# A fourth tile in the turn of right sides of the Strassen steps of a feed-forward block

## The chip, the cores and the metric

The kernel runs on one core of one Trainium2 chip. The metric is the device time of one execution in microseconds (us), as the median of several runs. The core's engines are named as the profile names them: PE multiplies matrices (PEld loads its weights), DVE and POOL work on vectors, ACT evaluates functions and copies, and SP issues the DMA transfers; each runs its own list of instructions in order.

## The reference

Two layers of a diffusion backbone run for two request groups of 1024 and 128 tokens that share all weights. Each layer is a mixer (a recurrence and a pooling in the first, latent attention in the second) and then a feed-forward block with a squared ReLU:

```python
D_MODEL = 1024
D_FF = 4 * D_MODEL

def sq_relu_mlp(h, w1, w2):
    return jnp.square(jax.nn.relu(h @ w1)) @ w2

...
        xs = xs + ms[5] * sq_relu_mlp(modulate(xs, p['g_ffn'], ms[3], ms[4]), p['ffn_w1'], p['ffn_w2'])
```

The change lies in the product with `w2`, which is computed once in each of the two layers.

## The kernel before

All tokens lie transposed: 1152 columns (1024 and 128) in NQ = 4 chunks of Q = 288. Every f32 factor is split into a high part, rounded to the multiplier's own f32r format, and a low part that is the rest; `mm3` (L165 to L168) then makes three matmuls, high by high, high by low and low by high. `split` (L157 to L163) makes the two parts: ACT copies the high part (L162), and DVE or POOL subtracts it to get the low one (L163).

`ffn` runs `up` for the first product, which squares its result and stores it to DRAM as high and low parts (`ad`) and unsplit (`ar`). The second product handles 14 of the 16 blocks of rows in seven **Strassen steps** of two blocks each, and the two others (`PLAIN`) directly. A step forms seven products, in the order of LATE: A11, A12, S3, A22, S2, S1, S4. Each is made for two halves g = 0 and 1, so a step has 14 **tiles** in a row, which are counted here from 0 to 13: A11 is tiles 0 and 1, A12 2 and 3, S3 4 and 5, A22 6 and 7, S2 8 and 9, S1 10 and 11, S4 12 and 13. One tile is 24 matmuls on PE, in four groups of six; each group fills a PSUM bank, which DVE adds to an accumulator (L881; in the first step ACT copies it, L877).

The right side of a tile is four [128, 288] pieces, high and low, in a buffer named `at` (4608 bytes per partition). Tiles 0 to 3, 12 and 13 (A11, A12, S4) are loaded from DRAM by `direct` (L852). Tiles 4 to 11 are sums that POOL makes in place in a tile `fb_b` (`right_sides`, L696), and `split` writes their parts into `at`. The buffers come from one turn, in which 14 tiles take three buffers one after the other:

```python
        four = lambda p, n=3: lambda: p.t([P, 2, 2, Q], F32R, tag="at", bufs=n)
...
        ats = cycle(four(fq))
```

A tile's load or split can begin when PE has finished with the tile that had the buffer before. The two `fb_b` tiles of the next step (L858, 1152 KB each) are loaded when the last splits of this step have read the old ones, and they stand on SP's queue ahead of the loads of tiles 12 and 13.

PE's order is the order of the code. The orders of DVE, ACT, POOL and SP are made when the kernel is built, by a scheduler with a model of the times; on the chip they are fixed. Memory on the left side is a stack: `fb`, then the accumulators, lie where the inputs of the first product lay. Layers 0 and 1 have the same code, with names that end in 0 and 1 (fq0, fq1).

Of the kernel before, what the change touches and what calls it, by code (L numbers as in the profile page):

```python
# [77 lines left out]
def emit(tc, A, O):  # L78
# [216 lines left out]
    def modulate(norm, x, c, hs, l, ffn, lo_eng=(po, ve), inplace=False, spare=None):  # L295
        scl = (sc_ffn if ffn else sc_mix)[l]
        sh0 = 24 if ffn else 0
        hh, hl = hs[c]
        for k in range(KT):
            xn = x[c][:, k, :]  # L300
            sh = lambda g: mod[l][:, sh0 + k, g:g + 1]
            if inplace:
                for a, b, g in groups(c, norm.ch):
                    ve.tensor_scalar(xn[:, a:b], xn[:, a:b], scl[:, k, g:g + 1], sh(g), op0=OP.mult, op1=OP.add)
                split(hh[:, k, :], hl[:, k, :], xn, eng=lo_eng[k % len(lo_eng)])
                continue
            xs = spare.t([P, norm.ch], tag="xn", bufs=2)
            for a, b, g in groups(c, norm.ch):
                ve.scalar_tensor_tensor(xs[:, a:b], xn[:, a:b], scl[:, k, g:g + 1], norm.rs[c][:, a:b],
                                        op0=OP.mult, op1=OP.mult)  # L310
            for a, b, g in groups(c, norm.ch):
                act(hh[:, k, a:b], xs[:, a:b], AF.Identity, bias=sh(g))
            for a, b, g in groups(c, norm.ch):
                ve.scalar_tensor_tensor(hl[:, k, a:b], xs[:, a:b], sh(g), hh[:, k, a:b].bitcast(F32),
                                        op0=OP.add, op1=OP.subtract)
# [402 lines left out]
    def slots_of(pools):  # L718

        while True:  # L720
            for s in pools:
                h = s.t([P, 1024], F32R, tag="hlh", bufs=3 if s is state["wl"] else 2)
                lo = s.t([P, 1024], F32R, tag="hll", bufs=3 if s is state["wl"] else 2)
                for i in range(2):
                    yield h[:, i * 512:(i + 1) * 512], lo[:, i * 512:(i + 1) * 512]
# [10 lines left out]
    def cycle(*makers):  # L736
        while True:
            for f in makers:
                yield f()
# [3 lines left out]
    def ffn(l, x, hs, hclose, tail, slow, then):  # L743

        fq = Scope(f"fq{l}", side="right")
# [5 lines left out]
        four = lambda p, n=3: lambda: p.t([P, 2, 2, Q], F32R, tag="at", bufs=n)  # L751
# [54 lines left out]

        fz = Scope(f"fz{l}", side="right")
        fb = Scope(f"fb{l}")
        raws = cycle(*[from_wp] * 3, lone(fx), lone(fz))
        slots = slots_of([fw, fw, state["wl"], state["wl"], state["wl"]])  # L810
        ats = cycle(four(fq))
        ae = Each(f"acc{l}")
        acc = {n: [ae.t([P, 4, Q]) for _ in range(2)] for n in ("A11", "S3", "A22", "S2", "S1", "S4", "A12")}

# [8 lines left out]
        def collect(name, g):  # L823

            t = {n: a[g] for n, a in acc.items()}
            add = lambda e, o, p, q: e.tensor_tensor(t[o], t[p], t[q], op=OP.add)  # L826
            if name == "A12":
                add(ve, "A12", "A12", "A11")
            elif name == "S3":
                gated(2 * g, 0, t["A12"])  # L830
            elif name == "S2":
                add(ve, "S2", "S2", "A11")
                add(po, "S3", "S3", "S2")
                add(po, "A22", "A22", "S3")
            elif name == "S1":
                add(po, "A11", "S3", "S1")
                add(ve, "S1", "S1", "S2")
                add(po, "S4", "S4", "S1")
                gated(2 * g, 1, t["A22"])
            elif name == "S4":  # L840
                gated(2 * g + 1, 1, t["A11"])
                gated(2 * g + 1, 0, t["S4"])

        todo = [s for s in range(ns) if s not in PLAIN]
        for s in todo[::2]:
# [15 lines left out]
            for name, o in LATE:  # L861
                ws = next(cw)
                for g in range(2):
# [18 lines left out]
                    if end:  # L882
                        collect(name, g)
        ae.close()
        fb.close()
        fp = Scope(f"fp{l}", side="right")
        then()
# [65 lines left out]
    def leave():  # L953
        ht.close()
        h0.close()

    ffn(0, x, hs, leave, Tail(nm, x, spill, lambda c, m: (po, ve)[c // 3], (5,) * 4), slow,
        lambda: hin.extend(chunk_pairs(hx, 4)))
    hs = hin
# [488 lines left out]

    end = Tail(nm, x, done, lambda c, m: ve if c == NQ - 1 else po, (5, 5, 5, 4))
    ffn(1, x, hs, leave, end, lambda *a: iter(()), lambda: None)  # L1450
    gain(NQ - 2)
    gain(NQ - 1)
# [130 lines left out]
```

## Time and profile before

| | |
|---|---|
| median of 3 runs | 2968.59 us (2967.73 to 2974.57) |
| the profiled execution | 2964.8 us |
| its span from first to last instruction | 2962.8 us |
| mean granted TensorE clock | 0.974 |
| busy share of the span | PE 94%, DVE 64%, ACT 46%, POOL 40% |

The profiled execution is one execution, and the rows below are of it. The Strassen steps lie at about 883 to 1212 us in layer 0 and 2590 to 2880 us in layer 1. A granted clock of 1.00 is 2.4 GHz and of 0.50 is 1.2 GHz. "Idle before" in a timeline row is the time for which the engine did nothing before that instruction, with what ended it behind the arrow.

### The profile page before, as it was taken

To read this page: it belongs to the slowest core of one execution; us is meant where nothing else is said; L and a number is where in the kernel's file an instruction comes from. 1 tells how busy PE (TensorE), PEld (TensorE's weight loads), DVE (VectorE), ACT (ScalarE), POOL (GpSimd) and SP (SyncE) were. 2 spreads that over 40 slices of the span, in tenths; PEclk is the share of its full clock that TensorE was granted. 3 is DMA by queue.
4 is the path that set the end of the run, shared out by engine and by line. 5 is a ranking of instruction groups with operands and counts; after the bars stand their busy time and mean duration, and the time that the engine had idled before them with its cause. 6 is when DMAs were issued, how large, how long until landed. Compare 5 with 4: busy or idle time off the path is not lost.

```text
span 2962.8 us, 51575 instructions
## 1 busy us (share of the span) xinstructions
PE 2791.4 (94%) x19896; PEld 2693.8 (91%) x19896; DVE 1910.7 (64%) x3518; ACT 1352.5 (46%) x3143; POOL 1187.8 (40%) x984
## 2 busy tenths in 40 slices
PE   5898799999999999899999999999999999999987
PEld 3886698999999999898999999988999999999987
DVE  5559677665656787875777777776831112377886
ACT  3356243222335222454777777773432223532335
POOL 3544111112157867624333233331011112777775
PEclk7999899999999999999999999999999999999998
DMA  5233414656655554420000000023244444555442
GB/s 225 94 120 103 167 51 166 217 207 215 219 188 175 181 172 158 136 81 21 20 15 21 14 15 23 23 91 109 85 172 156 151 163 151 187 169 173 153 158 88
DMA packets 144941, 372.78 MB, mean 126 GB/s; under 512 B 15944, under 2 KB 49080, under 8 KB 143288
## 3 DMA queue, kind: packets, MB, share of 16 engines
q1 hardware_dynamic: 144696, 369.50, 36.7%
q8 instruction: 156, 2.56, 0.4%
q14 instruction: 89, 0.73, 0.1%
HBM read 260.68 MB, written 108.75 MB: 125 GB/s over the span
## 4 chain that ended last, share of the span: by engine, by line
PE 76%; DVE 9%; DMA 4%; ACT 4%; POOL 3%; issue 3%; SPq 0%; DVEq 0%; ACTq 0%; POOLq 0%
PE ps_b L166 19%; PE ps_b L167 19%; PE ps_b L168 19%; PE pS_o L1145 3%; PE pS_t L1127 3%; DMA fq_at<-dram_t 3%; PE pS_s L166 3%; PE pS_s L168 2%; PE pS_s L167 2%; ACT aw_p L1120 1%; POOL acc_t L826 1%; PE pS_g L166 1%; PE pS_g L168 1%; PE pS_g L167 1%; ACT aw_ph L1131 1%
## 5 line engine op out<-in xcount | busy, mean ns | idle before, releaser
L765 POOL TENSOR_TENSOR fu_r<-fu_r 128x576 f32<-128x576 f32 x128 | 159.9, 1249 | 670.1 <-ACT fu_ah L764 647.3
L167 PE MATMUL ps_b<-ht_t,wl_hlh 128*128 128x288 f32 (+1 forms) x1312 | 404.9, 309 | 13.7 <-DVE ht_t L163 9.1
L166 PE MATMUL ps_b<-ht_t,wl_hlh 128*128 128x288 f32 (+1 forms) x1312 | 407.9, 311 | 7.3 <-ACT ht_t L162 5.0
L168 PE MATMUL ps_b<-ht_t,wl_hll 128*128 128x288 f32 (+1 forms) x1312 | 402.6, 307 | 0.0
L881 DVE TENSOR_TENSOR acc_t<-ps_b,acc_t 128x288 f32<-128x288 f32 x656 | 278.1, 450 | 94.6 <-PE ps_b L168 91.0
L766 DVE TENSOR_TENSOR fu_ah<-fu_r,fu_ah 128x576 fp32r<-128x576 f32 (+1 forms) x128 | 90.2, 705 | 358.9 <-POOL fu_r L765 358.9
L166 PE MATMUL ps_b<-fq_at,wl_hlh 128*128 128x288 f32 x1024 | 308.1, 301 | 12.1 <-DMA fq_at<-dram_t 12.1
L168 PE MATMUL ps_b<-fq_at,wl_hll 128*128 128x288 f32 x1024 | 305.3, 298 | 4.8 <-POOL wl_hll L163 4.8
L167 PE MATMUL ps_b<-fq_at,wl_hlh 128*128 128x288 f32 x1024 | 304.5, 297 | 0.0
L759 ACT ACTIVATE fu_r<-ps_b 128x288 f32<-128x288 f32 x256 | 103.9, 406 | 434.3 <-PE ps_b L168 431.0
L166 PEld LDWEIGHTS ps_b<-ht_t,wl_hlh 128*128 128x128 f32 x1312 | 250.0, 191 | 22.7 <-issue 5.8
L167 PEld LDWEIGHTS ps_b<-ht_t,wl_hlh 128*128 128x128 f32 x1312 | 250.4, 191 | 16.9 <-DVE ht_t L163 10.5
L162 ACT ACTIVATE wl_hlh<-w_raw 128x1024 fp32r<-128x1024 f32 (+1 forms) x161 | 137.3, 860 | 274.8 <-PE ps_b L167 230.6
L1135 DVE TENSOR_TENSOR aw_pl<-pS_t,aw_ph 128x384 fp32r<-128x384 f32 (+1 forms) x400 | 200.2, 540 | 83.0 <-ACT aw_ph L1131 77.4
L168 PEld LDWEIGHTS ps_b<-ht_t,wl_hll 128*128 128x128 f32 x1312 | 250.9, 191 | 0.0
L166 PE MATMUL ps_b<-fq_at,fw_hlh 128*128 128x288 f32 x736 | 221.7, 301 | 11.3 <-DMA fq_at<-dram_t 9.4
L1120 ACT ACTIVATE aw_p<-pS_s,aw_nb 128x384 f32<-128x384 f32 (+1 forms) x400 | 224.7, 579 | 15.2 <-DVE aw_nb L1114 14.3
L167 PE MATMUL ps_b<-fq_at,fw_hlh 128*128 128x288 f32 x736 | 220.3, 299 | 6.1 <-DVE fq_at L163 6.1
L1110 DVE TENSOR_REDUCE aw_mx<-pS_s 128x1 f32<-128x384 f32 (+1 forms) x400 | 203.3, 537 | 31.9 <-PE pS_s L168 30.7
L168 PE MATMUL ps_b<-fq_at,fw_hll 128*128 128x288 f32 x736 | 219.5, 298 | 0.0
L1131 ACT ACTIVATE aw_ph<-pS_t 128x384 fp32r<-128x384 f32 (+1 forms) x400 | 173.5, 486 | 83.7 <-PE pS_t L1127 83.4
L166 PEld LDWEIGHTS ps_b<-fq_at,wl_hlh 128*128 128x128 f32 x1024 | 196.8, 192 | 13.3 <-issue 10.9
(381 smaller groups left out, 8557.5 us busy)
## 6 DMA issues: line engine op xcount, KB each, us to landing
fq_at<-dram_t SPq DMA_DIRECT2D x96, 576.0 KB, 4.1
dram_t<-fu_ah SPq DMA_DIRECT2D x72, 576.0 KB, 2.8
w_raw<-in_ffn SPq DMA_DIRECT2D x64, 512.0 KB, 3.7
dram_t<-fu_r SPq DMA_DIRECT2D x112, 288.0 KB, 2.1
fb_b<-dram_t SPq DMA_DIRECT2D x28, 1152.0 KB
fq_at<-in_w_mod SPq DMA_DIRECT2D x128, 192.0 KB, 3.9
w_raw<-in_l_ffn_w SPq DMA_DIRECT2D x40, 512.0 KB, 4.6
w_raw<-in_w_mod SPq DMA_DIRECT2D x32, 512.0 KB, 4.2
```

What stands on the lines that cost most here:

```text
L162: act(hi, src, AF.Copy)
L166: mm(out, wh, hh, start=start, stop=False)
L167: mm(out, wh, hl, start=False, stop=False)
L168: mm(out, wl, hh, start=False, stop=stop)
L759: act(r[:, i ^ j, :], b[:, :Q], AF.Relu)
L765: po.tensor_tensor(r, r, r, op=OP.mult)
L766: ve.tensor_tensor(t[:, :, 1, :], r[:, :n, :], t[:, :, 0, :].bitcast(F32), op=OP.subtract)
L881: ve.tensor_tensor(to, b, to, op=OP.add)
L1110: ve.tensor_reduce(self.mx[:, i:i + 1], self.sc[i][0], axis=AX.X, op=OP.max)
L1120: act(self.pt[i][:, :w], v, AF.Exp, bias=self.nb, accum_out=lsum[:, self.h, self.blk, i:i + 1])
L1131: act(hi[g][:, :self.nks[g], j * P:(j + 1) * P], self.tp[g], AF.Copy)
L1135: ve.tensor_tensor(lo[g][s_], self.tp[g], hi[g][s_].bitcast(F32), op=OP.subtract)
```

## The change

The turn of `at` buffers gets a fourth member, a single tile from a pool `fr` of its own on the left side, which opens behind `fb` and closes with it. Of every four tiles three take the old buffers and one the new. A tile now follows the one four places back in its buffer, where it was three. The accumulators move up by 4608 bytes. No instruction is added or taken away on any engine, and PE's order stays.

```diff
         fb = Scope(f"fb{l}")
+        fr = Scope(f"fr{l}")
         raws = cycle(*[from_wp] * 3, lone(fx), lone(fz))
         slots = slots_of([fw, fw, state["wl"], state["wl"], state["wl"]])
-        ats = cycle(four(fq))
+        ats = cycle(*[four(fq)] * 3, four(fr, 1))
...
         ae.close()
+        fr.close()
         fb.close()
```

On DVE, in the second step of layer 0 (all middle steps read alike), the low parts of tiles 9, 10 and 11 (`fq0_at`, from `fb0_b_4`, `fb0_b_3` and `fb0_b_4`) stand among the additions of the banks (`acc05` is A22 of g = 1, that is tile 7; `acc06` and `acc07` are tiles 8 and 9). Before:

```order
L881 TENSOR_TENSOR acc05_t_1_8475<-ps_b_431_9352,acc05_t_1_8475 128x288
L163 TENSOR_TENSOR fq0_at_72_9427<-fb0_b_4_9080,fq0_at_72_9427 128x2x288
L881 TENSOR_TENSOR acc05_t_1_8475<-ps_b_432_9360,acc05_t_1_8475 128x288
...
L881 TENSOR_TENSOR acc06_t_1_8479<-ps_b_436_9403,acc06_t_1_8479 128x288
L163 TENSOR_TENSOR fq0_at_73_9470<-fb0_b_3_9074,fq0_at_73_9470 128x2x288
L881 TENSOR_TENSOR acc06_t_1_8479<-ps_b_437_9411,acc06_t_1_8479 128x288
...
L881 TENSOR_TENSOR acc07_t_1_8483<-ps_b_439_9430,acc07_t_1_8483 128x288
L163 TENSOR_TENSOR fq0_at_74_9505<-fb0_b_4_9080,fq0_at_74_9505 128x2x288
L881 TENSOR_TENSOR acc07_t_1_8483<-ps_b_440_9438,acc07_t_1_8483 128x288
```

The same place with the change:

```order
L882 TENSOR_TENSOR acc04_t_1_8474<-ps_b_428_9328,acc04_t_1_8474 128x288
L163 TENSOR_TENSOR fr0_at_6_9430<-fb0_b_4_9083,fr0_at_6_9430 128x2x288
L882 TENSOR_TENSOR acc04_t_1_8474<-ps_b_429_9336,acc04_t_1_8474 128x288
...
L882 TENSOR_TENSOR acc05_t_1_8478<-ps_b_431_9355,acc05_t_1_8478 128x288
L163 TENSOR_TENSOR fq0_at_67_9473<-fb0_b_3_9077,fq0_at_67_9473 128x2x288
L882 TENSOR_TENSOR acc05_t_1_8478<-ps_b_432_9363,acc05_t_1_8478 128x288
...
L882 TENSOR_TENSOR acc06_t_1_8482<-ps_b_436_9406,acc06_t_1_8482 128x288
L163 TENSOR_TENSOR fq0_at_68_9508<-fb0_b_4_9083,fq0_at_68_9508 128x2x288
L882 TENSOR_TENSOR acc06_t_1_8482<-ps_b_437_9414,acc06_t_1_8482 128x288
```

Each split stands one place in the turn earlier: that of tile 10 stands where tile 9's stood, behind tile 7's first bank, and that of tile 11 where tile 10's stood. On SP the order of the loads is the same in every step but the first, where the load of tile 3 moves ahead of two stores of the first product.

In the last step of layer 0 DVE also has the additions of whole accumulators (L826) and of these to x (L821). Before, around the low part of tile 6 (`fq0_at_139`):

```order
L163 TENSOR_TENSOR fq0_at_138_12050<-fb0_b_14_11850,fq0_at_138_12050 128x2x288
...
L821 TENSOR_TENSOR x0_t_1_2348<-x0_t_1_2348,acc012_t_1_8503 128x1152
L826 TENSOR_TENSOR acc013_t_1_8507<-acc013_t_1_8507,acc01_t_1_8459 128x1152
L881 TENSOR_TENSOR acc02_t_1_8463<-ps_b_700_12021,acc02_t_1_8463 128x288
L881 TENSOR_TENSOR acc02_t_1_8463<-ps_b_701_12029,acc02_t_1_8463 128x288
L163 TENSOR_TENSOR fq0_at_139_12096<-fb0_b_13_11844,fq0_at_139_12096 128x2x288
```

With the change tile 6 is `fq0_at_117` and tile 7 `fr0_at_23`:

```order
L163 TENSOR_TENSOR fq0_at_117_12099<-fb0_b_13_11847,fq0_at_117_12099 128x2x288
...
L822 TENSOR_TENSOR x0_t_1_2348<-x0_t_1_2348,acc012_t_1_8506 128x1152
L827 TENSOR_TENSOR acc013_t_1_8510<-acc013_t_1_8510,acc01_t_1_8462 128x1152
L882 TENSOR_TENSOR acc02_t_1_8466<-ps_b_700_12024,acc02_t_1_8466 128x288
L882 TENSOR_TENSOR acc02_t_1_8466<-ps_b_701_12032,acc02_t_1_8466 128x288
L163 TENSOR_TENSOR fr0_at_23_12134<-fb0_b_14_11853,fr0_at_23_12134 128x2x288
```

The low part of tile 6 now stands ahead of the two long additions, and that of tile 7 behind them.

On POOL, between the second and the third step, a low part of the weights of S3 of the third step (`fw0_hll_16`) and the first sums in the newly loaded `fb0_b_5` change places. Before:

```order
L163 TENSOR_TENSOR fw0_hll_16_9786<-w_raw_100_9620,fw0_hlh_15_9785 128x512
L696 TENSOR_TENSOR fb0_b_5_9628<-fb0_b_5_9628 128x2x288 x2
L696 TENSOR_TENSOR fb0_b_6_9634<-fb0_b_6_9634 128x2x288
```

With the change:

```order
L696 TENSOR_TENSOR fb0_b_5_9631<-fb0_b_5_9631 128x2x288 x3
L163 TENSOR_TENSOR fw0_hll_16_9789<-w_raw_100_9623,fw0_hlh_15_9788 128x512
L696 TENSOR_TENSOR fb0_b_6_9637<-fb0_b_6_9637 128x2x288
```

Three sums, which need the loaded tile, now stand ahead of the low part.

## Rows read from the trace of the kernel before

**Rows 1.** The page: span, and busy time of PE.
```profile
span 2962.8 us, 51575 instructions
...
PE 2791.4 (94%) x19896; PEld 2693.8 (91%) x19896; DVE 1910.7 (64%) x3518; ACT 1352.5 (46%) x3143; POOL 1187.8 (40%) x984
```

**Rows 2.** PE's waits, 870:1205 (layer 0): us in total, times, longest.
```profile
PE ps_b L166 <- DMA fq_at<-dram_t: 11.0, 5, 2.8
PE ps_b L167 <- DVE fq_at L163: 3.0, 1, 3.0
```

**Rows 3.** PE's waits, 2580:2880 (layer 1).
```profile
PE ps_b L166 <- DMA fq_at<-dram_t: 9.7, 5, 2.4
PE ps_b L167 <- DVE fq_at L163: 3.2, 1, 3.2
```

**Rows 4.** PE's timeline at three waits of layer 0.
```profile
967.98 0.38 PE L166 MATMUL ps_b<-fq_at,wl_hlh 128*128 128x288 f32 x1 [1.74 <-DMA fq_at<-dram_t]
...
1160.31 0.37 PE L166 MATMUL ps_b<-fq_at,fw_hlh 128*128 128x288 f32 x1 [2.77 <-DMA fq_at<-dram_t]
...
1189.04 0.40 PE L167 MATMUL ps_b<-fq_at,fw_hlh 128*128 128x288 f32 x1 [2.96 <-DVE fq_at L163]
```

**Rows 5.** SP's timeline: loads of fb_b, then of tiles 12 and 13.
```profile
957.35 2.14 SPq L858 DMA_DIRECT2D fb_b<-dram_t  x2
959.93 0.36 SPq L852 DMA_DIRECT2D fq_at<-dram_t  x1
...
963.10 0.36 SPq L852 DMA_DIRECT2D fq_at<-dram_t  x1
```

**Rows 6.** Windows: busy us (count) of PE, PEld, DVE, ACT, POOL; PEclk; DMA share, GB/s.
```profile
958.00:960.00 2.00, 2.00 (x18) 2.00 (x16) 1.88 (x6) 0.14 (x1) 0.00 (x0) 1.00 0.79 147
...
966.00:968.00 2.00, 0.26 (x3) 0.07 (x2) 1.59 (x2) 1.15 (x2) 1.88 (x3) 1.00 1.05 399
```

**Rows 7.** Windows of 7 us around waits, in both layers.
```profile
1014.00:1021.00 7.00, 6.00 (x34) 6.03 (x35) 2.03 (x5) 0.00 (x0) 7.00 (x6) 0.76 0.38 137
...
1158.00:1165.00 7.00, 4.69 (x35) 4.73 (x36) 3.52 (x7) 0.59 (x2) 7.00 (x6) 1.00 0.51 177
1188.00:1195.00 7.00, 5.96 (x33) 5.96 (x34) 7.00 (x14) 3.74 (x8) 1.49 (x1) 0.76 0.33 93
...
2731.00:2738.00 7.00, 5.59 (x31) 5.62 (x32) 2.18 (x5) 0.09 (x1) 7.00 (x6) 0.76 0.38 141
```

**Rows 8.** DVE's timeline, second step: low parts of tiles 9, 10 and 11.
```profile
951.58 1.39 DVE L163 TENSOR_TENSOR fq_at<-fb_b,fq_at 128x576 fp32r<-128x576 f32 x1
...
955.55 1.77 DVE L163 TENSOR_TENSOR fq_at<-fb_b,fq_at 128x576 fp32r<-128x576 f32 x1
...
958.34 0.74 DVE L163 TENSOR_TENSOR fq_at<-fb_b,fq_at 128x576 fp32r<-128x576 f32 x1
```

**Rows 9.** Windows from wait to wait: the first and the last of four.
```profile
967.98:1015.00 47.02, 44.69 (x336) 44.49 (x337) 36.63 (x70) 13.34 (x22) 36.55 (x25) 1.00 0.53 175
...
1111.35:1160.31 48.96, 46.19 (x337) 45.99 (x337) 37.70 (x70) 13.24 (x22) 33.67 (x24) 0.97 0.51 171
```

**Rows 10.** DVE's timeline in the last step of layer 0.
```profile
1183.41 1.81 DVE L821 TENSOR_TENSOR x_t<-x_t,acc_t 128x1152 f32<-128x1152 f32 x1
1185.15 2.44 DVE L826 TENSOR_TENSOR acc_t<-acc_t,acc_t 128x1152 f32<-128x1152 f32 x1
```

**Rows 11.** First step of layer 0: SP's last store of `up`, ACT's copy of tile 3.
```profile
891.38 0.32 SPq L767 DMA_DIRECT2D dram_t<-fu_ah  x1
...
895.61 1.00 ACT L877 ACTIVATE acc_t<-ps_b 128x288 f32<-128x288 f32 x3
```

**Rows 12.** PE's waits, 1205:1250, behind the last step of layer 0.
```profile
PE ps_b L280 <- POOL nt_acc L270: 5.8, 1, 5.8
```

**Rows 13.** POOL's timeline: a low part of S3's weights, the first sum.
```profile
961.09 1.30 POOL L163 TENSOR_TENSOR fw_hll<-w_raw,fw_hlh 128x512 fp32r<-128x512 f32 x1 [4.38 <-ACT fw_hlh L162]
963.42 1.43 POOL L696 TENSOR_TENSOR fb_b<-fb_b 128x576 f32<-128x576 f32 x1 [1.03 <-DMA fb_b<-dram_t]
```

## The prediction

> **What bounds the kernel now.** I read the page first: PE is busy for 2791.4 of 2962.8 us [rows 1], so a change of buffers can gain only where PE waits. PE's waits in the stretch of the Strassen steps come next: in layer 0 five waits for the load of an `at` tile, 11.0 us together, and one of 3.0 us for a low part made by DVE [rows 2]; in layer 1 five of 9.7 us and one of 3.2 us [rows 3]. The timeline puts the first of the five at 967.98 and the last at 1160.31 [rows 4]; they come once a step, at tile 12.
>
> SP's timeline shows why. The load of tile 12 goes at 959.93, when PE has finished tile 9, and the next at 963.10, one tile (3.17 us) later [rows 5]. Two tiles cover it, 6.3 us, and PE gets it at 967.98, after 8.05 us: the wait is 1.74 us, so PE was ready at 966.24. The load takes that long because of what is ahead of it: the two `fb_b` loads go at 957.35 and, as the second of the pair (2.14 us in all, 0.38 us for an issue), at 959.11. Together 2 x 1.18 MB + 0.59 MB = 2.95 MB must move; from about 959.3 the DMA engines are full (share 1.05, 399 GB/s) [rows 6]. At 400 GB/s that ends 7.4 us later, at 966.7, and PE sees it 1.3 us after that.
>
> A wait also costs clock. In the 7 us around the wait at 1015 the mean granted clock is 0.76 [rows 7]: a part runs at 1.2 GHz instead of 2.4, and 0.24 x 7 = 1.7 us are lost. Two more waits of layer 0 and two of layer 1 (2731 is one) look the same; the other five, 1160 among them, keep 1.00. Five times 1.7 is 8.5 us.
>
> **The change part by part.** No instruction comes or goes; buffers and four orders move.
>
> *Splits on DVE.* The `fb_b` loads wait for the low parts of tiles 10 and 11. In the trace these are at 955.55 (1.77 us) and 958.34 (0.74 us), tile 9's at 951.58 (1.39 us) [rows 8]; their ends, 957.32 and 959.08, are the two issues above. By the order, tile 10's low part now stands where tile 9's stood and tile 11's where tile 10's stood, each with its buffer free one tile earlier too. So the first `fb_b` load goes at about 953.0 (4.35 us earlier), the second at 957.35 (1.8 us earlier).
>
> *The load of tile 12.* It now waits for tile 8, done at 959.93 - 3.17 = 956.8, but SP issues it behind the second `fb_b` load, at 957.8: 2.1 us earlier. The first `fb_b` starts to move at 955.0 and is through at 957.9; from 959.3 only 1.18 + 0.59 = 1.77 MB move, 4.4 us, to 963.7, and PE sees the tile at 965.0. It needs it at 966.24. The landing moves 3.0 us against PE, more than the longest of the ten waits, 2.77 us [rows 4]. Bounds: if only the second issue's 1.8 us counted, about 20.7 - 10 x 1.8 = 2.7 us, say 3, of the ten waits would stay; less than none cannot. I take all ten as gone, **20.7 us**, since the queue's own bytes say 3.0. Tile 13's load follows with 0.59 MB, to 966.5, for use at 966.24 + 3.17 = 969.4.
>
> *The clock.* With no wait the five low stretches go: **8.5 us**. Between all and none I take all, because each sits right behind one of these waits; none is the lower bound.
>
> *What must keep up.* A step without waits is 14 tiles; 336 matmuls take 44.69 busy us [rows 9], so 44.7 to 44.8. DVE's 36.6 to 37.7 us a step and POOL's 33.7 to 36.6 fit, at 84% and 82%. What is gained in steps 2 to 6 is therefore kept: everything behind shifts.
>
> *The last step.* PE's wait of 2.96 us at 1189.04 is for tile 6's low part, which stood behind additions of 1.81 and 2.44 us [rows 10]; behind it 1.7 us of clock go in layer 0 [rows 7], none in layer 1. The low part now stands ahead of the additions. But DVE is full there (7.00 of 7 us), and one more low part ahead of the same additions keeps the banks of tiles 4 to 6 waiting: eight banks at 0.8 us are 6.4 us of cover. I expect PE to wait for a bank, or for tile 7's low part, instead. Of 2.96 + 1.7 + 3.15 = 7.8 us the gain is between 0 and 7.8; I take **2 us**, near the end where DVE's work sets the pace.
>
> *The first step.* Tile 3 loads sooner, into memory that PE left before; before, it was in time too. The accumulator of tile 3 moves onto the last buffer of the first product: ACT's copy at 895.61 must follow the store issued at 891.38 [rows 11]. 4.2 us lie between; if the store took longer, ACT would hold, with banks as cover. Nothing, at worst 1 us.
>
> The sum is 20.7 + 8.5 + 2 = 31.2 us against the profiled 2964.8: 2933.6. The runs' median is 3.8 us above the profiled execution, so I say 2937.
>
> **The rivals.** *The load is bound by bytes, not by its issue.* The Trainium skill, "DMA: Bandwidth & Descriptors", section "Queues, rings and completion order", says that each DMA engine takes descriptors in ring order. By that rule a buffer that frees a load earlier is worth only what the bytes ahead of it leave. The trace agrees as far as tile 12 lands when all 2.95 MB have moved. As a mechanism here: the second `fb_b` gains 1.8 us, and if the first gains no more than that, 3 us of waits stay; if these still bring the clock down, all 8.5 us stay lost. The gain is 20.7 - 3 = 17.7 us, 2951. Against it stands the first `fb_b`'s 4.35 us. 12%.
>
> *Given back behind the loop.* PE waits 5.8 us for POOL's sums of squares after the last step [rows 12]. Were POOL's work the path through all the steps, that wait would grow by what PE gains: no change, 2960 to 2969. POOL idles over 10 us in each step [rows 9], which speaks against it. 7%, with the case that the scheduler's order brings nothing.
>
> *Slower.* On POOL three sums, 1.43 us each, and the wait for the `fb_b` load now stand ahead of a low part of S3's weights, which was done at 962.4 [rows 13]. Were it needed at once, PE would wait some 4.3 us a step, 12 times, 52 us: 2968.6 - 31 + 52 = 2990. It is needed at tile 4 of the next step, 967.98 + 6 x 3.2 = 987.2. It decides only from a delay of 24.8 us on; 4.3 us and a load's 8 us are far below. 5%.
>
> **How the numbers follow.** The forecast has 71%. The remaining 5% are for more: the whole 7.8 us of the last steps in place of 2, and the waits behind them, to 39 us, 2929. A measurement of this kernel can tell 0.3%, 8.9 us. Faster: 71 + 12 + 5 = 88%; the same 7%; slower 5%. The range takes in the larger gain and the first rival with some scatter of the runs: 2927 to 2955.
>
> **What the changed profile would show.** PE's five waits for `fq_at` or `fr_at` loads in each layer gone or below 1 us; the clock 1.00 from the second to the sixth step; steps of 44.8 us; the second `fb_b` and tile 12's load issued some 2 us earlier against PE's tile 12; the wait at tile 6 of the last step shorter, or at a bank or tile 7. POOL's wait for S3 would show the slower rival. The prediction is wrong if tile 12 still comes late though its buffer is free, or if the time gained in the steps comes back as a longer wait of PE behind the loop.

## The result and the profile after

The changed kernel takes 2938.69 us (median of 4 runs, 2937.71 to 2940.58) against 2970.29 us for the kernel before on the same chip (2967.73 to 2974.57): a ratio of 0.9893, 95% interval 0.9876 to 0.991, or 31.6 us less by the medians. The forecast was 2937. The profiled execution is the fastest of the four, 2937.71 us; all rows of this section are of it unless the text says otherwise. One execution of 7228 us, in the first run with the buffer at tile 12 alone, is far off all others and is left out of that run's median and ratio.

The page's first part, which answers to [rows 1]: with the same number of matmuls PE is busy for 8.7 us less, and the span is 26.9 us shorter.

```profile
span 2935.9 us, 51561 instructions
PE 2782.7 (95%) x19896; PEld 2686.6 (92%) x19896; DVE 1898.9 (65%) x3518; ACT 1354.0 (46%) x3143; POOL 1203.6 (41%) x984
```

PE's waits in the stretches of the steps, 870 to 1205 and 2560 to 2880, which answer to [rows 2, 3] (us in total, times, longest), and below them the wait behind the loops, at 1205 to 1250 and 2880 to 2900:

```profile
PE ps_b L166 <- DVE acc_t L882: 4.3, 2, 2.7
...
PE ps_b L166 <- DVE acc_t L882: 4.9, 3, 2.7
...
PE ps_b L280 <- POOL nt_acc L270: 8.3, 1, 8.3
...
PE ps_b L280 <- POOL nt_acc L270: 6.5, 1, 6.5
```

No wait for a load is left, and none for a low part. In their place stand waits for a bank, all five in the last steps. Behind the loop of layer 0 the wait for POOL's sums is longer than the 5.8 us of [rows 12], but two other waits that stood there before are gone:

```profile
PE ps_b L168 <- POOL wl_hll L163: 1.7, 1, 1.7
PE ps_b L166 <- DMA fq_at<-dram_t: 0.8, 1, 0.8
```

So PE waits there for 8.3 us in all, before and after. Behind layer 1, from 2880 to the end, it is 10.9 us before and 10.8 after.

Windows of one step each, from tile 12 to tile 12 (the first and the last of four), which answer to [rows 9]; then 7 us around tile 12 of the fifth step of layer 1 (at 2732.41 before, with a clock of 0.76 behind it) and around the two bank waits of 2.67 us, which answer to [rows 7]:

```profile
967.49:1011.95 44.46, 44.46 (x338) 44.46 (x337) 35.95 (x69) 13.15 (x22) 39.48 (x27) 1.00 0.56 185
...
1100.81:1145.21 44.40, 44.40 (x339) 44.40 (x337) 37.20 (x69) 13.38 (x22) 34.65 (x23) 1.00 0.55 181
...
2709.00:2716.00 7.00, 7.00 (x55) 7.00 (x55) 4.54 (x10) 1.16 (x2) 7.00 (x6) 1.00 0.74 220
1193.00:1200.00 7.00, 4.33 (x23) 4.11 (x22) 7.00 (x11) 2.58 (x6) 5.70 (x3) 0.76 0.44 160
2848.00:2855.00 7.00, 4.35 (x22) 4.35 (x23) 7.00 (x13) 1.82 (x4) 5.70 (x3) 0.78 0.14 28
```

A middle step is 44.4 us with PE busy throughout and a clock of 1.00; it was 47.0 to 49.0. DVE's 36.0 to 38.2 us and POOL's 34.7 to 39.5 us a step still fit.

DVE's low parts of tiles 10 and 11 of the second step, then SP's timeline behind them, which answer to [rows 8] and [rows 5]:

```profile
953.27 0.74 DVE L163 TENSOR_TENSOR fq_at<-fb_b,fq_at 128x576 fp32r<-128x576 f32 x1
...
956.97 1.43 DVE L163 TENSOR_TENSOR fq_at<-fb_b,fq_at 128x576 fp32r<-128x576 f32 x1
```

```profile
954.04 4.76 SPq L859 DMA_DIRECT2D fb_b<-dram_t  x2
...
958.43 0.38 SPq L859 DMA_DIRECT2D fb_b<-dram_t  x1
958.91 0.41 SPq L853 DMA_DIRECT2D fq_at<-dram_t  x1
```

PE's timeline at the start of tile 10 before the change, and then with it; at tile 12; and at two bank waits of the last step:

```profile
959.73 0.29 PE L166 MATMUL ps_b<-fq_at,wl_hlh 128*128 128x288 f32 x1
...
961.15 0.29 PE L166 MATMUL ps_b<-fq_at,wl_hlh 128*128 128x288 f32 x1
...
967.49 0.34 PE L166 MATMUL ps_b<-fq_at,wl_hlh 128*128 128x288 f32 x1
...
1173.70 0.40 PE L166 MATMUL ps_b<-fq_at,fw_hlh 128*128 128x288 f32 x1 [1.66 <-DVE acc_t L882]
...
1196.90 0.61 PE L166 MATMUL ps_b<-fq_at,wl_hlh 128*128 128x288 f32 x1 [2.67 <-DVE acc_t L882]
```

To read these beside the rows of before, place them by PE: tile 10 starts at 961.15 here, and at 959.73 before. Less these 1.4 us, the first `fb_b` load goes at 952.6, the second at 957.0 and that of tile 12 at 957.5; the prediction said 953.0, 957.35 and 957.8. The ends of the two low parts, 954.01 and 958.40, are again the two issues of `fb_b`. Tile 12 starts without a wait. The trace also records when a transfer has landed: tile 12's load was complete at 967.33, only 0.16 us ahead of PE; in steps 3 to 6 of this layer and 2 to 6 of the other it was 0.9 to 1.7 us ahead.

In the last step DVE's timeline shows what PE now waits for:

```profile
1167.43 0.74 DVE L163 TENSOR_TENSOR fq_at<-fb_b,fq_at 128x576 fp32r<-128x576 f32 x1
...
1170.82 2.45 DVE L827 TENSOR_TENSOR acc_t<-acc_t,acc_t 128x1152 f32<-128x1152 f32 x1
1173.20 0.81 DVE L882 TENSOR_TENSOR acc_t<-ps_b,acc_t 128x288 f32<-128x288 f32 x2
...
1193.04 3.44 DVE L827 TENSOR_TENSOR acc_t<-acc_t,acc_t 128x1152 f32<-128x1152 f32 x1
1196.40 2.27 DVE L882 TENSOR_TENSOR acc_t<-ps_b,acc_t 128x288 f32<-128x288 f32 x6
```

The low part of tile 6 starts early, at 1167.43, but the banks stand behind the whole additions of 2.45 and 3.44 us: the first bank behind each is free about 0.4 us after the addition ends, and there PE goes on. Windows of the whole last step, in layers 0 and 1 before the change, then with it:

```profile
1166.75:1215.96 49.21, 46.25 (x339) 46.02 (x338) 47.06 (x74) 18.35 (x34) 32.90 (x19) 0.97 0.48 150
2834.80:2882.51 47.71, 44.56 (x339) 44.33 (x337) 45.95 (x74) 18.36 (x34) 33.15 (x19) 1.00 0.43 134
...
1151.55:1203.09 51.54, 47.13 (x339) 45.99 (x337) 47.30 (x74) 18.16 (x34) 36.20 (x20) 0.97 0.41 133
2804.60:2857.05 52.45, 47.51 (x339) 46.32 (x338) 47.53 (x74) 19.11 (x37) 37.04 (x21) 0.97 0.36 111
```

The last step did not become shorter. It is 2.3 us longer in layer 0 and 4.7 us in layer 1, and DVE, the third number behind the length, is busy for 46 to 47.5 us of it in all four.

### The profile page after: what moved, and what is told of

Same layout as the page of the kernel before. It is cut to its first block, busy times and chain, and to the rows that moved or that the text cites. A ratio compares the mean times of both kernels' runs of the same rounds, so it can differ in the third digit from the quotient of the medians.

```text
span 2935.9 us, 51561 instructions
## 1 busy us (share of the span) xinstructions
PE 2782.7 (95%) x19896; PEld 2686.6 (92%) x19896; DVE 1898.9 (65%) x3518; ACT 1354.0 (46%) x3143; POOL 1203.6 (41%) x984
## 5 line engine op out<-in xcount | busy, mean ns | idle before, releaser
L882 DVE TENSOR_TENSOR acc_t<-ps_b,acc_t 128x288 f32<-128x288 f32 x656 | 269.8, 448 | 51.9 <-PE ps_b L168 49.9
L166 PE MATMUL ps_b<-fq_at,wl_hlh 128*128 128x288 f32 x800 | 239.4, 299 | 6.0 <-DVE acc_t L882 6.0
L168 PE MATMUL ps_b<-fq_at,wl_hll 128*128 128x288 f32 x800 | 236.7, 296 | 0.0
L167 PE MATMUL ps_b<-fq_at,wl_hlh 128*128 128x288 f32 x800 | 236.3, 295 | 0.0
L1112 DVE TENSOR_REDUCE aw_mx<-pS_s 128x1 f32<-128x384 f32 (+1 forms) x400 | 203.5, 539 | 31.6 <-PE pS_s L168 30.4
L163 DVE TENSOR_TENSOR wl_hll<-w_raw,wl_hlh 128x1024 fp32r<-128x1024 f32 (+1 forms) x109 | 139.3, 1279 | 100.5 <-ACT wl_hlh L162 99.3
L696 POOL TENSOR_TENSOR fb_b<-fb_b 128x576 f32<-128x576 f32 x112 | 175.8, 1581 | 25.0 <-DMA fb_b<-dram_t 19.8
L166 PE MATMUL ps_b<-fq_at,fw_hlh 128*128 128x288 f32 x576 | 172.1, 299 | 3.4 <-DVE acc_t L882 3.3
L167 PE MATMUL ps_b<-fq_at,fw_hlh 128*128 128x288 f32 x576 | 170.2, 295 | 0.0
```

Of the source, the lines that this page charges most:

```text
L163: eng.tensor_tensor(lo, src, hi.bitcast(F32), op=OP.subtract)
L166: mm(out, wh, hh, start=start, stop=False)
L167: mm(out, wh, hl, start=False, stop=False)
L168: mm(out, wl, hh, start=False, stop=stop)
L696: po.tensor_tensor(a[:, :, o, :], a[:, :, p, :], a[:, :, q, :], op=op)
L882: ve.tensor_tensor(to, b, to, op=OP.add)
```

## The experiments

Every ratio is to the kernel before on the same chip. Theory: a load of tile 12 is late by the bytes that stand ahead of it on the queue, and the fourth buffer lets the splits, and so the `fb_b` loads, go earlier. The main rival: its own place of issue is what counts.

**Fourth buffer for the splits alone.**

```diff
-        ats = cycle(*[four(fq)] * 3, four(fr, 1))
+        ats = cycle(*[four(fq)] * 4, four(fr, 1), *[four(fq)] * 3, four(fr, 1), *[four(fq)] * 5)
```

> The fourth buffer serves tiles 4 and 8 alone. Every split of tiles 5 to 11 follows the tile four places back, as in the change, and the low parts of tiles 10 and 11 stand on DVE where the change has them, so the loads of fb_b go early; but the loads of tiles 12, 13, 0, 1 and 2 follow the tile three places back, as in the kernel before: the load of tile 12 again cannot be issued before PE is done with tile 9, two tiles (6.3 us) ahead of its use. Theory (the bytes ahead of it on the queue decide): with the fb_b loads about 2 us or more earlier the 0.59 MB land 3.0 us earlier although they are issued at the old place; no wait above 0.3 us at tile 12, time as with the change, 2937 to 2941. Rival (the place of its issue decides): the ten waits of together 20.7 us and most of the 8.5 us of clock stay, 2962 to 2969.

Measured: 2936.33 us (2933.43 to 2937.17), ratio 0.9876 (0.9862 to 0.989). The theory holds; the wait of 0.56 us that is left at tile 12 is for a bank. SP's timeline of the second step:

```profile
953.32 5.33 SPq L859 DMA_DIRECT2D fb_b<-dram_t  x2
960.82 0.36 SPq L853 DMA_DIRECT2D fq_at<-dram_t  x1
```

and PE at tile 12 of that step, with all of layer 0's waits up to 1205 below:

```profile
967.68 0.41 PE L166 MATMUL ps_b<-fq_at,wl_hlh 128*128 128x288 f32 x1 [0.56 <-DVE acc_t L882]
```

```profile
PE ps_b L166 <- DVE acc_t L882: 4.9, 3, 2.7
PE ps_b L168 <- POOL wl_hll L163: 1.3, 1, 1.3
```

Tile 12's load is issued 6.30 us before PE is through with tile 11 (967.68 - 0.56 - 960.82), as before, and PE starts the tile 6.86 us after the issue, behind a bank; before, 8.05 us went by. The landing itself, by the trace's record, came 6.60 us after the issue in this step and 4.6 to 5.7 us in the four behind it, where it took 7.9 to 9.0 before. So in this step the load still landed 0.3 us after PE could have had it, which the wait for the bank hides; in the others of layer 0 it was early. The place of its own issue is not what the change had to move; that the `fb_b` loads went earlier was enough. The 2 us by which this kernel lies under the change are within the intervals.

**Fourth buffer for tile 12 alone**, twice.

```diff
+        ats = cycle(*[four(fq)] * 12, four(fr, 1), four(fq))
```

> The fourth buffer serves tile 12 alone, so its load is issued a step ahead, in front of the fb_b loads. Tiles 4 to 11 keep three buffers, and the orders of DVE and POOL are row for row those of the kernel before; only this load moves on SP. Tile 13 follows tile 9, so its load is issued where that of tile 12 was, lands 8.05 us later and is needed 9.5 us later: no wait. Theory (the waits of the steps are worth 20.7 us and their clock 8.5 us, and nothing else changes by it): 2968.6 - 29.2 = 2939, with the waits of the last step (3.0 us in layer 0, 3.2 us in layer 1 for a low part of DVE) as before. Rival (the early splits and fb_b loads are needed too, or the early load delays another): waits of 1 us and more at tile 13 or at tiles 0 to 4, 2950 to 2969.

> The fourth buffer for tile 12 alone once more, for a profile of it. Its times were 2940 to 2949 with 2939 expected. Theory (the ten waits are gone and what is above 2939 is scatter of the clock elsewhere): no wait of PE above 0.5 us for a load in steps 2 to 6. Rival (the splits three places back and the late fb_b loads leave waits): waits at tile 13 or at tiles 0 to 5 that add up to some 5 us with their clock.

Measured: 2944.6 us (median of five, 2940.22 to 2949.30), ratio 0.9908 (0.9893 to 0.9923); then 2940.85 us (2940.13 to 2942.6), 0.9906 (0.9893 to 0.9919). PE's waits of the second run in both layers:

```profile
PE ps_b L167 <- DVE fq_at L163: 5.0, 3, 3.9
PE ps_b L166 <- DMA fq_at<-dram_t: 0.4, 1, 0.4
...
PE ps_b L167 <- DVE fq_at L163: 3.9, 1, 3.9
PE ps_b L168 <- POOL wl_hll L163: 2.8, 1, 2.8
```

With the order of DVE and POOL of the kernel before, the ten waits go too: the load stands in front of the `fb_b` loads. So either way of getting bytes out of the queue ahead of it is enough alone. The rival (late splits are needed elsewhere) fails in the steps; but the wait for the low part in the last step stays, and grows from 2.96 to 3.95 us: DVE starts that low part 23.7 us behind the start of the step, where it was 21.5. The 5 us that the first of the two runs had above 2939 are mostly its chip: the kernel before takes 2972.15 us there and 2968.68 us on the chip of the second, so the gain is 27.6 and 27.8 us, for the 29.2 expected.

**Layer 0 alone.**

```diff
+        ats = cycle(*[four(fq)] * 3, *[four(fr, 1)] * (l == 0))
```

> The fourth buffer is used in layer 0 only; layer 1 has the turn of three. Theory (each layer's gain stands for itself and is kept): layer 0 keeps its five waits of 11.0 us and three dips of 1.7 us gained, 16.1 us, and layer 1 loses 9.7 and 3.4, 13.1 us: 2968.6 - 16.1 = 2952 to 2953, with the waits of layer 1 as in the kernel before. Rival (part of what layer 0 gains is given back behind the loop, up to layer 1, or layer 1's gain has another source): below 2948 or above 2958.

Measured: 2951.55 us (2950.43 to 2956.94), ratio 0.9933 (0.9921 to 0.9946). The time is what the theory said; against the kernel before on the same chip it is 20.6 us less (16.0 to 23.5 by the interval), where the theory has 16.1, so the time tells little, and the profile more. PE's waits of layer 1, where the turn of three is left:

```profile
PE ps_b L166 <- DMA fq_at<-dram_t: 11.4, 6, 2.6
PE ps_b L167 <- DVE fq_at L163: 3.0, 1, 3.0
...
```

In it PE takes 267.2 us for the first six steps of layer 0 (283.9 before, 266.5 with the change) and 283.4 us for those of layer 1 (281.8 before, 266.7 with the change). Each layer's gain stands for itself.

**Whole additions taken ahead of the last step**, to test whether DVE and POOL pace it. `gated` gets a place for its product; `collect` and the banks change so:

```diff
             if name == "A12":
-                add(ve, "A12", "A12", "A11")
-            elif name == "S3":
-                gated(2 * g, 0, t["A12"])
+                gated(2 * g, 0, t["A11"], t["A12"])
...
-                add(po, "S4", "S4", "S1")
...
-                gated(2 * g + 1, 0, t["S4"])
+                gated(2 * g + 1, 0, t["S1"])
...
-                        elif end and name == "S4":
-                            accum(x, b, m, 2 * g + 1, gate)
+                        elif s >= todo[{"A12": -2, "S4": -4}.get(name, 0)] and name in ("A12", "S4"):
+                            accum(x, b, m, 2 * g + (name == "S4"), gate)
...
+                    elif s == todo[{"A12": -4, "S4": -6}.get(name, 0)] and name in ("A12", "S4"):
+                        gated(2 * g + (name == "S4"), 0, acc[name][g])
```

> The change, and in each layer four scaled additions of whole accumulators to x are taken ahead of the last step: A12's is made in the sixth step and S4's in the fifth, and their banks of the steps behind go straight to x. In the last step DVE loses the two additions of A11 to A12 and POOL the two of S1 to S4 (1.4 to 3.4 us each in the trace of the changed kernel); DVE has two additions more in the fifth step and two in the sixth, where it idles some 7 us a step. Theory (what is left of the last step's waits, 1.7 and 2.7 us for banks and 8.3 us for POOL's sums of squares in layer 0, and 0.6, 1.7, 2.7 and 6.5 us in layer 1, is paced by the work on DVE): 3 to 7 us a layer gained, 2925 to 2933. Rival (POOL's own sums of squares or the long way from x through ACT to POOL set the wait, not the amount of work): within 3 us of 2938.7. Or the fifth and sixth step become full on DVE, and PE waits there for banks: 2940 or more.

Measured: 2929.77 us, ratio 0.9864 (0.9845 to 0.9882), within the 2925 to 2933 of the theory, but in two groups: 2928.51, 2929.12 and 2929.77, and 2940.95 and 2943.17. The profiled execution is the slowest. In it PE's wait for POOL behind the loop of layer 0 is 2.8 us instead of 8.3, and 6.5 us are lost in the last step to one low part of weights on DVE that took 8.60 us, where such parts take 0.7 to 2.7 us elsewhere. Below it POOL's instruction of that time:

```profile
1161.25 8.60 DVE L163 TENSOR_TENSOR fw_hll<-w_raw,fw_hlh 128x512 fp32r<-128x512 f32 x1 [3.10 <-ACT fw_hlh L162]
...
1168.03 1.27 POOL L163 TENSOR_TENSOR fw_hll<-w_raw,fw_hlh 128x512 fp32r<-128x512 f32 x1
```

POOL works without a gap from 1149.49 to 1169.30, and the low part on DVE ends 0.55 us later, at 1169.85. That would fit a DVE that could not go on beside POOL, but no run tests it, and the cause stays open.

**The same, one addition a step; then with A22 too.**

```diff
+        EARLY = {("A12", 0): todo[2], ("A12", 1): todo[4], ("S4", 0): todo[6], ("S4", 1): todo[8]}
...
+                        elif s > EARLY.get((name, g), s):
```

For the second, `EARLY` has A22 too, and POOL's addition of S3 to A22 goes:

```diff
+        EARLY = {("A22", 0): todo[2], ("A22", 1): todo[4], ("A12", 0): todo[4], ("A12", 1): todo[6], ("S4", 0): todo[6], ("S4", 1): todo[8]}
...
-                add(po, "A22", "A22", "S3")
+                gated(2 * g, 1, t["S3"], t["A22"])
```

> As the early sums before, but the four scaled additions of whole accumulators to x are made one a step, behind the second step (A12 of g = 0), the third (A12 of g = 1), the fourth (S4 of g = 0) and the fifth (S4 of g = 1), and the banks of the steps behind each go straight to x. Theory (DVE's and POOL's sums pace the last step; the early sums gained 9 us, and had waits for the load of tile 12 and for banks in the sixth and seventh step of layer 0 where two additions stood close together): no wait for a load, PE's wait for POOL's sums of squares behind the loop below 5 us in layer 0 (8.3 with the change), 2924 to 2930. Rival (the last step is not paced by these sums): 2936 to 2941.

> As the run before it, and A22 is treated in the same way: scaled and added to x behind the second step (g = 0) and the third (g = 1), its later banks straight to x (A12 one step later than there, S4 as one step earlier for g = 0 and g = 1). In the last step POOL loses two more whole additions of each layer (S3 to A22, 2.7 to 3 us each); DVE's number of additions there stays. Theory A (POOL's additions are on the path of the last step together with DVE's): 3 to 6 us less than the run before it. Theory B (DVE alone paces it): within 2 us of the run before it.

Measured: 2933.5 us (2927.67 to 2945.02), ratio 0.9871 (0.9857 to 0.9886), and 2938.98 us (2930.43 to 2945.28), 0.9899 (0.9884 to 0.9914). Both expectations missed: "no wait for a load" for the first, whose time lies between the ranges of its two theories, and neither theory gave 5 us more for the second. In the second PE's wait behind the loop of layer 0 is gone, but PE waits 3.2 us for POOL's low part of weights instead, 4.2 us for loads and 5.3 us for banks in layer 0: that POOL's additions were one pace-maker among several is read from these waits and not tested alone. The first run's third step shows why loads are late again. DVE, then SP, then PE at tile 12:

```profile
995.11 2.08 DVE L823 TENSOR_TENSOR x_t<-x_t,acc_t 128x1152 f32<-128x1152 f32 x1
...
1005.06 0.75 DVE L163 TENSOR_TENSOR fq_at<-fb_b,fq_at 128x576 fp32r<-128x576 f32 x1
```

```profile
1005.84 2.87 SPq L858 DMA_DIRECT2D fb_b<-dram_t  x2
1008.80 4.25 SPq L852 DMA_DIRECT2D fq_at<-dram_t  x3
```

```profile
1016.64 0.37 PE L166 MATMUL ps_b<-fq_at,fw_hlh 128*128 128x288 f32 x1 [0.78 <-DMA fq_at<-dram_t]
```

The addition stands in front of low parts; the first `fb_b` load then goes 10.0 us before PE is ready for tile 12 (1015.86), where the change gave it 12.6 us in the same step (999.38 to 1011.95).

**Three runs on one chip: spread additions with the buffer at tile 12; the change again; early additions with the buffer at the splits.** The turns are those of the first two experiments.

> The four early sums spread over the steps, with the fourth buffer for tile 12 alone: its load goes ahead of the fb_b loads and no longer hangs on the low parts of tiles 10 and 11. Theory (the waits for loads of the two spread runs come from early sums that hold up a low part on DVE, and by it an fb_b load and the load of tile 12 behind it): no wait for a load in steps 2 to 6, the short bank waits of 0.5 to 1 us stay, and the low parts of the last step are waited for again by 1 to 4 us; 2930 to 2936. Rival (the loads are late for another reason): waits of 0.8 to 2.4 us at tile 12 or 13 stay.

> The change itself once more, on the chip of the two runs beside it. Both theories: 2936 to 2941, no wait of PE for a load in the steps.

> The early sums in the fifth and sixth step with the fourth buffer at tiles 4 and 8 only. The splits follow four places back, the load of tile 12 three places. Theory (bytes ahead of it decide, and in the sixth step the early sums hold the low parts back): waits for the load of tile 12 of 1 to 3 us in the sixth step alone, 2926 to 2934, under the change by 5 us or more. Rival (the early sums bring nothing that the change keeps): within 3 us of the change.

Measured: 2932.43 us (2929.62 to 2937.66), ratio 0.9872 (0.9854 to 0.989), within the 2930 to 2936 expected; the change 2940.68 (2939.17 to 2942.45), 0.9896 (0.9878 to 0.9914); and 2932.63 (2931.04 to 2933.83), 0.987 (0.9855 to 0.9886). PE's waits of the first in layer 0:

```profile
PE ps_b L167 <- DVE fq_at L163: 1.7, 3, 1.1
PE ps_b L166 <- DVE x_t L352: 1.6, 1, 1.6
...
```

No wait for a load: once tile 12's load does not stand behind `fb_b`, delayed low parts do no harm there, which bears out the queue's part in the chain of the run before. The third expected waits for loads in the sixth step and had none, only bank waits up to 2.5 us and, behind the steps, one of 2.0 us in either layer for POOL's low part of weights; its time is the one expected. The change itself, expected without any, had one wait for a load this time (0.83 us at 2626, tile 12 of the second step of layer 1), so its cover is thin. Both variants lie 8 us under the change on the same chip; every one of their eight times is below its four. Their intervals against the kernel before still touch that of the change. Windows of the last step of layer 0, in the change and in the third:

```profile
1153.26:1204.06 50.80, 45.88 (x339) 44.73 (x337) 45.95 (x74) 18.12 (x34) 35.49 (x20) 1.00 0.42 135
...
1157.10:1202.86 45.76, 44.75 (x339) 44.52 (x338) 41.61 (x75) 17.67 (x33) 33.98 (x20) 1.00 0.53 163
```

With 4.3 us of DVE's work taken out, the last step is 5.0 us shorter (7.3 us in layer 1); the third's turn of buffers without early additions had 50.2 and 51.5 us. So the work on DVE and POOL, the engines that lost the additions, sets the pace of this step. The sixth step pays for it: 47.7 and 49.7 us in the two layers, 44.4 with the change.

## Why the prediction was right

The forecast of 2937 us was met, and the cause that it named is the right one. But of its terms two were wrong in opposite directions, so that the sum came out so well is in part luck.

Where the time came from, by the start of the same matmul on PE in the two profiled executions (us; PE's order is the same, and a step has 336 matmuls):

| PE starts | before | after | difference |
|---|---|---|---|
| the first step, layer 0 | 882.89 | 885.08 | +2.2 |
| the second step | 928.13 | 929.37 | +1.2 |
| the last step | 1166.75 | 1151.55 | -15.2 |
| the work behind the steps | 1215.96 | 1203.09 | -12.9 |
| its sums L280 | 1245.52 | 1230.92 | -14.6 |
| the first step, layer 1 | 2552.99 | 2537.92 | -15.1 |
| the second step | 2599.09 | 2582.21 | -16.9 |
| the last step | 2834.80 | 2804.60 | -30.2 |
| the work behind the steps | 2882.51 | 2857.05 | -25.5 |
| its sums L280 | 2911.38 | 2882.75 | -28.6 |
| end of the span | 2962.83 | 2935.90 | -26.9 |

- *Ten waits and five dips of the clock, 20.7 + 8.5 = 29.2 us.* Right. Steps 2 to 6 of layer 0 gained 16.4 us, for which the prediction's terms give 11.0 + 3 x 1.7 = 16.1; those of layer 1 gained 13.3, for 9.7 + 2 x 1.7 = 13.1. That the dips hung on the waits is seen in the windows: from 967 to 1150 and from 2600 to 2800 the clock is 1.00 with the change. With layer 1 left as it was, its waits and its time stayed.
- *The path by which the load comes sooner.* Right in kind. The issues came within 0.4 us of those worked out. The prediction counted both the first `fb_b` load's 4.35 us and the place of tile 12's own issue; the splits alone show that the bytes ahead decide, and tile 12 alone that leaving the queue's tail is enough too. The 3.0 us by which the landing was to move are not what the step that it was worked out for shows: there it moved by 1.9 us, counted from PE's start of tile 10 (8.11 us behind it before, 6.18 with the change), in the nine others by 2.5 to 4.0. From 954 to 960 the DMA engines moved 213 to 283 GB/s in that step, not the 400 of the prediction. That all ten waits went is no proof of the 3.0: in that step it was close.
- *The first step, for which the prediction has no gain.* It gained 1.0 us in layer 0 and 1.8 in layer 1. Its tile 12 also waited for its load before, 0.56 and 1.38 us, but the profile puts these waits down to ACT, and so they were not counted:

```profile
921.71 0.37 PE L166 MATMUL ps_b<-fq_at,fw_hlh 128*128 128x288 f32 x1 [0.56 <-ACT fw_hlh L162]
...
2592.64 0.37 PE L166 MATMUL ps_b<-fq_at,fw_hlh 128*128 128x288 f32 x1 [1.38 <-ACT acc_t L877]
```

  By the record of landings these two loads were complete at 921.57 and 2592.50, 0.14 us ahead of PE, which is also the distance at the ten waits that the profile does put down to loads.
- *The last step, a gain of 2 us out of 0 to 7.8.* Wrong in sign. That PE would wait for a bank instead of the low part, with DVE full (7.00 of 7 us around the wait, before and after), was right. But the bank waits and the low clock behind one of them cost more than what they replaced: the step grew by 2.3 and 4.7 us. The work behind it became 1.7 and 3.2 us shorter, so 2.2 us in all were lost where 2 us of gain were forecast. Early additions, which take work from DVE and POOL here, shorten the step, to 45.8 and 44.5 us in the last run, and the wait for POOL behind the loop to 2.2 to 4.8 us (none in one of the runs).
- *Sum.* 29.8 + 2.8 - 2.2 = 30.4 us for 31.2: the two errors nearly cancel. The two profiled executions differ by 27.1 only, since the one of after had lost 2.2 us ahead of the first step and 1.7 us behind PE's last sums. The medians differ by 31.6 because the profiled execution of before was 5.5 us below its median here, and that of after 1.0 us; the prediction carried over 3.8 us for this. Between the medians and the terms there is thus room for several us that no run settles.
- *The rivals.* "Bound by bytes" expected 3 us of waits to stay, because the first `fb_b` would gain no more than the second; it went 4.7 us earlier, for the 4.35 that its row said. Its premise, that what is ahead in the queue decides, is what the first experiment confirms. The Trainium skill, "DMA: Bandwidth & Descriptors", section "Queues, rings and completion order", has descriptors taken in ring order; the trace agrees: with the issue at an unchanged 6.30 us ahead, PE has the tile 6.86 us after it where it was 8.05. "Given back behind the loop" did not occur: PE's waits there are as long in all as before, and what was lost was lost in the last step. "Slower by POOL's order" did not occur: the low part of S3's weights ran at 966.75, behind three sums, some 19 us ahead of its use.

```profile
962.01 4.78 POOL L696 TENSOR_TENSOR fb_b<-fb_b 128x576 f32<-128x576 f32 x3
966.75 1.30 POOL L163 TENSOR_TENSOR fw_hll<-w_raw,fw_hlh 128x512 fp32r<-128x512 f32 x1
```

## What to carry to other kernels

A late load is judged by the bytes that stand ahead of it on its queue and by when these could start: a buffer that frees an earlier, larger transfer can be worth more than one for the late load itself, and a load taken out of the tail of the queue is worth as much. When a wait goes, look at the engine that is full at that place: in the steps, where DVE was at 84%, all of the gain was kept; in the last one, where it was full, the wait took another name and became longer. Work moved into idle time of such an engine must not stand in front of what releases a transfer. The name that the profile gives a short wait can be another's: the two waits of the first steps, put down to ACT, ended with a load.

## What the runs showed that was not expected

The clock's answer to a wait is not fixed. The wait of 2.67 us for a bank in the last step of layer 0 was followed by a low stretch in the profiled execution of the change (0.76 in the window at 1193), and by none in that of its second run. That run's wait, and its window:

```profile
1199.20 0.40 PE L166 MATMUL ps_b<-fq_at,wl_hlh 128*128 128x288 f32 x1 [2.67 <-DVE acc_t L882]
```

```profile
1195.00:1202.00 7.00, 4.33 (x33) 4.09 (x32) 7.00 (x11) 2.85 (x6) 5.71 (x3) 1.00 0.46 160
```

So 1.7 us at each wait is a price that comes or stays away between executions of one program at one place. The forecast's five dips were counted in one execution and are the number of that one: where layer 1 kept the turn of three, its five waits had three low stretches (0.76 in the windows at 2621, 2669 and 2717), and two in the kernel before. Eleven executions of the kernel before on one chip go from 2965.16 us with a mean clock of 0.975 to 2977.21 us with 0.970.
